# Split input-projection weights kept in DRAM after their first use, in a hybrid decoder layer

## The chip, the core and the metric

The kernel runs on one core of one Trainium2 chip. The metric is the device time of one execution in microseconds (us); less is better. The engines are named as the profile names them: PE is TensorE's matmul, PEld its weight load, DVE is VectorE, ACT is ScalarE, POOL is GpSimd, and SP is the queue that issues every DMA of this kernel.

## The reference

One decoder layer on a sequence of 2048 tokens with a width of 1024, all in float32. The input is normalised, one projection `w_in` makes 4224 columns of it, three branches use the columns, and one output projection adds their result to the input.

```python
h = rmsnorm(x, norm_g[l])
p = h @ w_in[l]
q, k, v, z_att, cb, cc, ch, z_conv, rw_p, z_rwkv = split_cols(p, sizes)
att = diff_attention(...)                    # 4 heads, two softmax maps each
cv = short_conv(cb, cc, ch, conv_w[l])
rw = rwkv7_time_mix(rw_p, ...)               # 4 heads of 64, recurrent
mixed = concatenate([att * silu(z_att), cv * silu(z_conv), rw * silu(z_rwkv)])
x = x + mixed @ w_out[l]
return rmsnorm(x, final_norm_g)
```

## The kernel before

**Tiles of the projection.** The 4224 columns are 33 tiles of 128. A tile's weights are `wr`, 128 partitions by 8 blocks by 128 columns, 512 KB. The product keeps float32 accuracy by splitting: `wh` is `wr` rounded to the matmul's type, `wl` is the rest, and `inproj` (L350) does three matmuls for each of 8 blocks, `wh` with the high part of h, `wh` with its low part, and `wl` with the high part (L357 to L359). One chunk is 512 tokens, so a tile and a chunk are 24 matmuls.

**Loads.** `load_w` (L333) fetches `wr` by one DMA (L326) and splits it: `wh` on ACT in the first stage (L340) and on POOL later (L343, two halves), `wl` on POOL always (L345, four quarters). `wr` has one buffer after the first stage; `wh` and `wl` have two each, so a tile's weights can be made while the tile ahead of it is used.

**How often.** The sequence is worked through in two halves of two chunks. Where a step list is run by `each`, one load serves both chunks; where it is run by `both` (L440), all tiles of chunk 0 come first and then all of chunk 1, with a load for each. So there are 85 loads of 33 tiles: 33 first ones and 52 later ones. The first loads are all in half 0. Run by `both` are six rwkv tiles in the first stage, the four tiles of attention head 3 in half 0 (named K3, V3, Q3 and ZA3 below, in this order), one rwkv tile of half 1, and the eight convolution tiles in half 1 (CC0, CH0, CB0, ZC0 and the same with 1).

**Order of the work.** The main line is: a first stage of projection alone, rwkv of half 0, attention of half 0, rwkv of half 1, attention of half 1, the output projection. While the middle four run, `filler` (L1265) feeds projection matmuls, four or five at a time, between theirs. PE's order is fixed by the program. The order on the other engines and on SP's queue comes from a scheduler that places an instruction where its own model says that it can run. Each engine and SP work strictly in that order: a DMA that waits for a semaphore holds all DMAs behind it.

**Names used.** `xt` are loads of x for the row sums of half 1 (L233), `QL`, `QH`, `K`, `V`, `zs` are loads for attention (L923 to L941, L1042), `pk_`, `pq_`, `pza_` are stores of projection results to DRAM (L370, L385), `P` are softmax tiles, L984 and L985 are the score matmuls, L1060 transposes the softmax tiles. `rs` and `hbc` (L304, L261) scale the first stage's results, `G`, `wu`, `bc` are rwkv matmuls.

Of the kernel before, what the change touches and what calls it, by code (L numbers as in the profile page):

```python
# [11 lines left out]
F32 = mybir.dt.float32  # L12
# [11 lines left out]
NK = 8  # L24
# [8 lines left out]
P = 128  # L33
# [112 lines left out]
def trunk(ctx, tc, a, o, phases="RTO"):  # L146
    nc = tc.nc
    mm = nc.tensor.matmul
    dma = nc.sync.dma_start
# [59 lines left out]
    def dtile(name, shape):  # L209
        return dr.tile(list(shape), F32, name=name)  # L210
# [12 lines left out]
    hl = [[None] * NK, [None] * NK]  # L223
# [95 lines left out]
    early_w, early_r = {}, {}  # L319

    def fetch_w(ti):
        if wpool[0] is not None:
            wr = wpool[0].tile([P, NK, P], F32, name="wr0", bufs=3)
        else:
            wr = ap.tile([P, NK, P], F32, name="wr", bufs=WRB)
        dma(wr, a["wt"][ti])  # L326
        return wr

    def parts(n):

        return [slice(i * NK // n, (i + 1) * NK // n) for i in range(n)]

    def load_w(ti):  # L333
        if ti in early_w:
            return early_w.pop(ti)
        wr = early_r.pop(ti) if ti in early_r else fetch_w(ti)
        wh = ap.tile([P, NK, P], F32R, name="wh", bufs=2)
        wl = ap.tile([P, NK, P], F32R, name="wl", bufs=2)
        if wpool[0] is not None or ON_ACT[0]:
            cpy(wh, wr)  # L340
        else:
            for ks in parts(2):
                nc.gpsimd.tensor_scalar(wh[:, ks], wr[:, ks], 1.0, 1.0, ALU.mult, ALU.mult)  # L343
        for ks in parts(4):
            nc.gpsimd.tensor_tensor(wl[:, ks], wr[:, ks], wh[:, ks].bitcast(F32), ALU.subtract)  # L345
        return wh, wl

    later = []

    def inproj(ti, evac, chunks):  # L350
        wh, wl = load_w(ti)
        for c in chunks:
            ps = pj(f"pj{ti}_{c}")
            flush = list(later)
            later.clear()
            n = 0
            for k in range(NK):  # L357
                for lhs, rhs in ((wh, hh), (wh, hl), (wl, hh)):
                    mm(ps, lhs[:, k], rhs[c][k], start=(n == 0), stop=(n == 3 * NK - 1))  # L359
                    n += 1  # L360
                    if n == 3 * NK:
                        evac(c, ps)
                    yield T512
                    if n == 6:
                        for f in flush:
                            f()
# [964 lines left out]
    with tc.tile_pool(name="st", bufs=1, side="right", reuse_waits="tile") as sp:  # L1331
        wpool[0] = sp
        r = rwkv_steps(0)
        order = (6, 2, 0, 4, 3, 1, 5)
        early_w[T_RW + order[0]] = load_w(T_RW + order[0])
        x0 = load_h0(0, sp)
        for i in order[1:3]:
# [4 lines left out]
        n = 0  # L1342
# [40 lines left out]
        for c in range(2):  # L1383
            for i, (f, args) in enumerate(two):
                ti = (T_RW + order[R0C], T_ZR)[i]
                if c == 0:
                    ws[ti] = load_w(ti)
                early_w[ti] = ws[ti]
                for _ in f(*args, (c,)):
                    pass  # L1390
# [19 lines left out]
    if "mix" in o:  # L1410
        for k in range(8):
            n = 256 if k < 4 else 512
# [43 lines left out]
```

## Time and profile before

| what | us |
|---|---|
| median of 3 runs | 1668.31 (1664.82 to 1672.17) |
| the profiled execution, its own time | 1671.53 |
| span of the profiled execution | 1669.4 |
| PE busy | 1547.7 |
| DVE busy | 948.0 |
| ACT busy | 743.6 |
| POOL busy | 669.9 |

The page slices the span into 40 parts and groups instructions by source line; the other views list an engine's instructions in time, who waited for whom, and the chain of work that ended last. A number in brackets behind a row, such as [2.63 <-DVE P L1030], is the idle time just ahead of the instruction and what ended it.

### The profile page before, as it was taken

What the parts mean: (1) busy time and instruction counts of PE and PEld (TensorE: products, weight loads), DVE (VectorE), ACT (ScalarE), POOL (GpSimd) and SP (SyncE); (2) the same over time, 40 slices, a digit from 0 to 9 for tenths busy, and PEclk for the clock granted to TensorE, in tenths of its full rate; (3) what the DMA queues carried; (4) which work ended last, traced back from release to release, by engine and by line L of the source; (5) the groups of instructions that cost most, each with busy time, mean ns of one, the idle gap of its engine ahead of it and who ended that gap; (6) DMA issues with size and microseconds to landing.
All of it is one profiled execution on the core that took longest, in us unless ns stands there. A gap on an engine that the chain in (4) does not pass through costs nothing.

```text
span 1669.4 us, 29369 instructions
## 1 busy us (share of the span) xinstructions
PE 1547.7 (93%) x10328; PEld 1209.9 (72%) x10328; DVE 948.0 (57%) x2355; ACT 743.6 (45%) x1903; POOL 669.9 (40%) x943
## 2 busy tenths in 40 slices
PE   5999999999998789999999999999989999997998
PEld 4777667677776667887666666778778878876786
DVE  7554765555325866763565554418776766666611
ACT  6432222322216555652322222216656777777732
POOL 4673534333234554344333223235543432321243
PEclk9999999999999898999999999999999999999999
DMA  6324222322266553324323222263343443331233
GB/s 220 101 89 147 61 71 67 89 82 89 76 196 207 174 188 103 98 77 134 98 87 97 80 82 78 79 196 101 111 127 98 145 143 99 109 101 37 73 101 114
DMA packets 147347, 184.70 MB, mean 111 GB/s; under 512 B 39520, under 2 KB 91776, under 8 KB 147200
## 3 DMA queue, kind: packets, MB, share of 16 engines
q1 hardware_dynamic: 147200, 182.82, 35.9%
q8 instruction: 82, 1.34, 0.3%
q14 instruction: 65, 0.53, 0.1%
HBM read 129.26 MB, written 53.48 MB: 109 GB/s over the span
## 4 chain that ended last, share of the span: by engine, by line
PE 54%; DVE 12%; DMA 7%; issue 6%; SPq 5%; POOL 4%; ACT 4%; DVEq 0%; POOLq 0%; ACTq 0%
PE pj L359 24%; PE ops L1232 8%; PE av L1052 6%; PE aT L1060 3%; PE S L984 2%; PE S L985 2%; POOL wl L345 2%; DMA wr<-in_wt_dram 2%; SPq L627 1%; DVE nm L990 1%; DVE tmpx L682 1%; DVE P L1030 1%; SPq L692 1%; DMA U<-ud 1%; ACT P L993 1%
## 5 line engine op out<-in xcount | busy, mean ns | idle before, releaser
L359 PE MATMUL pj<-hh,wh 128*128 128x512 f32 x1008 | 420.9, 418 | 16.8 <-POOL wh L343 11.6
L359 PE MATMUL pj<-hh,wl 128*128 128x512 f32 x1008 | 418.4, 415 | 0.7 <-POOL wl L345 0.5
L359 PE MATMUL pj<-hl,wh 128*128 128x512 f32 x1008 | 418.1, 415 | 0.0
L345 POOL TENSOR_TENSOR wl<-wr,wh 128x256 fp32r<-128x256 f32 x340 | 274.6, 837 | 46.2 <-ACT wh L340 44.1
L993 ACT ACTIVATE P<-S,nm 128x512 f32<-128x512 f32 (+3 forms) x320 | 200.2, 627 | 131.1 <-DVE nm L990 120.8
L990 DVE TENSOR_REDUCE nm<-S 128x1 f32<-128x512 f32 (+3 forms) x320 | 192.7, 607 | 82.3 <-PE S L985 78.7
L359 PEld LDWEIGHTS pj<-hh,wh 128*128 128x128 f32 x1008 | 192.8, 191 | 57.5 <-POOL wh L343 12.9
L359 PEld LDWEIGHTS pj<-hh,wl 128*128 128x128 f32 x1008 | 192.7, 191 | 42.9 <-issue 3.4
L359 PEld LDWEIGHTS pj<-hl,wh 128*128 128x128 f32 x1008 | 192.5, 191 | 39.2 <-issue 2.9
L343 POOL TENSOR_SCALAR wh<-wr 128x512 fp32r<-128x512 f32 x140 | 88.7, 651 | 233.7 <-PE pj L359 148.8
L1052 PE MATMUL av<-aTf,V 128*128 128x256 f32 x576 | 150.8, 386 | 0.0
L984 PE MATMUL S<-K,QH 128*128 128x512 f32 (+2 forms) x320 | 125.3, 392 | 26.7 <-ACT P L993 26.2
L1030 DVE SCALAR_TENSOR_TENSOR P<-P,sc 128x512 f32<-128x512 f32 (+3 forms) x160 | 114.2, 745 | 20.0 <-ACT P L1020 13.2
L985 PE MATMUL S<-K,QL 128*128 128x512 f32 (+2 forms) x320 | 118.5, 370 | 0.0
L1052 PEld LDWEIGHTS av<-aTf,V 128*128 128x128 f32 x576 | 103.0, 193 | 10.8
L1232 PE MATMUL ops<-woh,wh 128*128 128x512 f32 x256 | 105.1, 410 | 5.5 <-ACT wh L1211 5.5
L1065 ACT COPY aTf<-aT 128x512 f32<-128x512 f32 x144 | 84.0, 586 | 57.3 <-PE aT L1060 56.9
L1232 PE MATMUL ops<-wol,wh 128*128 128x512 f32 x256 | 106.1, 414 | 0.0
L1232 PE MATMUL ops<-woh,wl 128*128 128x512 f32 x256 | 105.4, 412 | 0.0
L989 DVE TENSOR_TENSOR S<-S,bt 128x256 f32<-128x256 f32 (+1 forms) x152 | 57.4, 378 | 80.8 <-PE S L985 77.3
L984 PEld LDWEIGHTS S<-K,QH 128*128 128x128 f32 x320 | 61.7, 193 | 51.0 <-ACT P L993 36.6
L1060 PE MATMUL aT<-con,P 128*128 128x128 f32 x576 | 89.6, 279 | 9.5 <-DVE P L1030 5.6
(337 smaller groups left out, 2471.3 us busy)
## 6 DMA issues: line engine op xcount, KB each, us to landing
wr<-in_wt_dram SPq DMA_DIRECT2D x85, 512.0 KB, 3.8
wr<-mx SPq DMA_DIRECT2D x128, 64.0 KB, 2.0
oxt<-in_x_dram SPq DMA_DIRECT2D x32, 256.0 KB, 3.1
out_dram<-oxt SPq DMA_DIRECT2D x32, 256.0 KB, 2.2
prw<-s SPq DMA_DIRECT2D x28, 256.0 KB, 2.0
V<-pv SPq DMA_DIRECT2D x24, 256.0 KB, 3.1
x<-in_xT_dram SPq DMA_DIRECT2D x16, 256.0 KB, 6.5
pv<-t SPq DMA_DIRECT2D x16, 256.0 KB, 2.1
```

What stands on the lines that cost most here:

```text
L343: nc.gpsimd.tensor_scalar(wh[:, ks], wr[:, ks], 1.0, 1.0, ALU.mult, ALU.mult)
L345: nc.gpsimd.tensor_tensor(wl[:, ks], wr[:, ks], wh[:, ks].bitcast(F32), ALU.subtract)
L359: mm(ps, lhs[:, k], rhs[c][k], start=(n == 0), stop=(n == 3 * NK - 1))
L984: mm(s[:, 0:sw], QH[:, m, off:off + P], K[:, m, 0:sw], start=True, stop=False)
L985: mm(s[:, 0:sw], QL[:, m, off:off + P], K[:, m, 0:sw], start=False, stop=True)
L990: nc.vector.tensor_reduce(nm[:, m, g:g + 1], s[:, 0:gw], AX.X, ALU.max, negate=True)
L993: act(p[:, 0:gw], s[:, 0:gw], AF.Exp, bias=nm[:, m, g:g + 1], accum_out=l[:, m, g:g + 1])
L1030: stt(pt[1, g][:, 0:gw], pt[1, g][:, 0:gw], sc[:, 1, g:g + 1], pt[0, g][:, 0:gw], ALU.mult, ALU.add)
L1052: mm(av[:, 0:256], Vs.get((h, kc))[:, ko:ko + P], tf[:, d * 256:d * 256 + 256], start=kb + d == 0, stop=kb + d == nb - 1)
L1060: nc.tensor.transpose(t[:, d * 256 + qi * P:d * 256 + qi * P + P], x["A"][g][:, ko:ko + P], ident)
L1065: cpy(tf, t)
L1232: mm(ps, l[:, k], Ws[n][r][k], start=(c == 0), stop=(c == 3 * NK - 1))
```

## The change

When a tile has been split for the first time, `wh` and `wl` are stored to two DRAM tiles (1 MB together). A later load of the same tile is two DMAs from there straight into `wh` and `wl`; it has no `wr`, and neither ACT nor POOL does anything for it.

```diff
+    wd = {}
+
     def load_w(ti):
+
         if ti in early_w:
             return early_w.pop(ti)
-        wr = early_r.pop(ti) if ti in early_r else fetch_w(ti)
         wh = ap.tile([P, NK, P], F32R, name="wh", bufs=2)
         wl = ap.tile([P, NK, P], F32R, name="wl", bufs=2)
+        if ti in wd:
+            for t, d in zip((wh, wl), wd[ti]):
+                dma(t.bitcast(F32), d)
+            return wh, wl
+        wr = early_r.pop(ti) if ti in early_r else fetch_w(ti)
         if wpool[0] is not None or ON_ACT[0]:
...
         for ks in parts(4):
             nc.gpsimd.tensor_tensor(wl[:, ks], wr[:, ks], wh[:, ks].bitcast(F32), ALU.subtract)
+        wd[ti] = [dtile(f"w{n}{ti}", (P, NK, P)) for n in "hl"]
+        for t, d in zip((wh, wl), wd[ti]):
+            dma(d, t.bitcast(F32))
         return wh, wl
```

In the changed program L355 is the store of a part, L343 its load, and every line behind the edit has a number higher by 10. PE's order is the same before and after. SP's order is not, and neither is POOL's.

SP's queue at the first load of V3 (`wr`, L326), in half 0 of attention, before. The rows ahead are for the tile ZA2 and attention, those behind are the loads of `QH` and `xt`:

```order
L370 DMA pza_0_5352<-th 128x512
L941 DMA QL_5139<-pq_1l 64x256
L326 DMA wr<-in_wt_dram 128x1024
L940 DMA QH<-pq_1h 64x256 x2
L233 DMA xt<-in_x_dram 128x512 x2
```

The same queue after the change, ahead of the same load of V3; `wl_5585` is the stored low part of K3:

```order
L355 DMA wl_5585<-wl 128x1024
L950 DMA QH<-pq_1h 64x256
L233 DMA xt<-in_x_dram 128x512
L950 DMA QH<-pq_1h 64x256
L233 DMA xt<-in_x_dram 128x512 x3
L950 DMA QH<-pq_1h 64x256
L951 DMA QL_5217<-pq_1l 64x256
L233 DMA xt<-in_x_dram 128x512 x2
L950 DMA QH<-pq_1h 64x256 x2
L233 DMA xt<-in_x_dram 128x512
L951 DMA QL_5218<-pq_1l 64x256
L233 DMA xt<-in_x_dram 128x512
```

In these twelve rows stand eleven of the `xt` loads, and no load of weights. The queue goes on with V3's load and what is behind it, and the store of a result for attention:

```order
L950 DMA QH<-pq_1h 64x256 x2
L233 DMA xt<-in_x_dram 128x512 x3
L951 DMA QL_5218<-pq_1l 64x256
L326 DMA wr<-in_wt_dram 128x1024
L395 DMA pk_0h<-thi 128x512
```

The load of V3 stood ahead of all sixteen `xt` loads and the `QH` loads among them; it now stands behind them, in the place that Q3's load had.

SP's queue where attention of half 1 begins, before. The second `wr` is CC0's load; the 21 loads of `K`, `QH`, `QL` and `V` begin behind it:

```order
L326 DMA wr<-in_wt_dram 128x1024
L370 DMA pv_2_12116<-t_12114 128x512
L370 DMA pv_3_12253<-t_12251 128x512
L830 DMA mx_3_139<-Y 128x256
L326 DMA wr<-in_wt_dram 128x1024
L923 DMA K<-pk_0h 64x512
L924 DMA K<-pk_0l 64x512
```

The same queue after the change, at the end of those 21 loads; `wh_1264` and `wl_1265` are CC0's stored parts, `wh_1362` and `wl_1363` are CH0's:

```order
L939 DMA V<-pv_0_3370 128x512
L395 DMA pq_2h<-thi 128x512
L395 DMA pq_2l<-tlo 128x512
L395 DMA pq_3h<-thi 128x512
L395 DMA pq_3l<-tlo 128x512
L380 DMA pza_2_12317<-th 128x512
L343 DMA wh<-wh_1264 128x1024
L343 DMA wl<-wl_1265 128x1024
L380 DMA pza_3_12347<-th 128x512
L343 DMA wh<-wh_1362 128x1024
L343 DMA wl<-wl_1363 128x1024
```

CC0's load stood ahead of the 21 loads; it now stands behind them and behind five stores.

SP's queue where CH0 is loaded for its second chunk, after the change:

```order
L343 DMA wh<-wh_1362 128x1024
L1196 DMA wor<-in_wo_dram 128x512 x5
L951 DMA QL_12205<-pq_2l 64x256
L493 DMA mx_2_130<-th 128x512
L950 DMA QH<-pq_2h 64x256 x2
L1196 DMA wor<-in_wo_dram 128x512
L950 DMA QH<-pq_2h 64x256 x2
L1196 DMA wor<-in_wo_dram 128x512 x2
L951 DMA QL_12205<-pq_2l 64x256
L343 DMA wl<-wl_1363 128x1024
```

Fourteen DMAs came between the two halves of this load.

## Rows read from the trace of the kernel before

**Rows 1.** The page's part 1: engine, busy us, share of the span, instructions.
```profile
PE 1547.7 (93%) x10328; PEld 1209.9 (72%) x10328; DVE 948.0 (57%) x2355; ACT 743.6 (45%) x1903; POOL 669.9 (40%) x943
```
**Rows 2.** Busy us (and instructions) of PE, PEld, DVE, ACT, POOL; PEclk, DMA share, GB/s.
```profile
0.00:20.00 20.00, 10.57 (x32) 6.44 (x33) 12.72 (x21) 15.86 (x26) 8.91 (x19) 1.00 0.88 306
...
480.00:645.00 165.00, 135.93 (x600) 108.79 (x599) 103.27 (x243) 86.30 (x234) 80.45 (x112) 0.90 0.60 183
```
**Rows 3.** Groups of the two POOL splits: busy us, mean ns of one, idle before.
```profile
L345 POOL TENSOR_TENSOR wl<-wr,wh 128x256 fp32r<-128x256 f32 x340 | 274.6, 837 | 46.2 <-ACT wh L340 44.1 <-PE pj L359 2.2
...
L343 POOL TENSOR_SCALAR wh<-wr 128x512 fp32r<-128x512 f32 x140 | 88.7, 651 | 233.7 <-PE pj L359 148.8 <-DMA wr<-in_wt_dram 71.4 <-DMA K<-pk_3l 8.3
```
**Rows 4.** Waits of PE, whole span: us in total, times, longest us.
```profile
PE pj L359 <- POOL wh L343: 11.6, 3, 5.5
```
**Rows 5.** Waits of PE in 600 to 660, 780 to 1060 and 1130 to 1300 us.
```profile
PE S L984 <- ACT P L993: 5.8, 2, 3.3
...
PE G L607 <- DVE KB L595: 3.1, 2, 1.6
PE wu L755 <- DVE Z L747: 2.7, 3, 1.5
...
PE S L984 <- ACT P L993: 7.1, 6, 3.7
```
**Rows 6.** SP's queue in time around V3's load: start us, us, engine line operation.
```profile
498.68 0.33 SPq L326 DMA_DIRECT2D wr<-in_wt_dram  x1
...
517.36 0.45 SPq L941 DMA_DIRECT2D QL<-pq_1l  x1
517.90 0.54 SPq L326 DMA_DIRECT2D wr<-in_wt_dram  x1
```
**Rows 7.** POOL in time: the split of the tile whose load was issued at 517.90.
```profile
523.42 1.20 POOL L343 TENSOR_SCALAR wh<-wr 128x512 fp32r<-128x512 f32 x2 [5.38 <-DMA wr<-in_wt_dram]
```
**Rows 8.** PE in time: V3's first matmul, two idle times behind it.
```profile
512.39 0.58 PE L359 MATMUL pj<-hh,wh 128*128 128x512 f32 x1
...
525.22 0.55 PE L1060 MATMUL aT<-con,P 128*128 128x128 f32 x3 [2.63 <-DVE P L1030]
...
568.67 0.79 PE L359 MATMUL pj<-hh,wh 128*128 128x512 f32 x1 [5.54 <-POOL wh L343]
```
**Rows 9.** SP's queue in time where attention of half 1 begins.
```profile
1091.41 0.37 SPq L326 DMA_DIRECT2D wr<-in_wt_dram  x1
...
1105.52 0.58 SPq L929 DMA_DIRECT2D V<-pv  x1
...
1108.31 0.52 SPq L370 DMA_DIRECT2D pza<-th  x1
1108.92 0.76 SPq L326 DMA_DIRECT2D wr<-in_wt_dram  x1
```
**Rows 10.** PE in time: the first matmul of CC0, and that of CH0.
```profile
1108.08 0.39 PE L359 MATMUL pj<-hh,wh 128*128 128x512 f32 x1
...
1117.51 0.79 PE L359 MATMUL pj<-hh,wh 128*128 128x512 f32 x1 [3.67 <-POOL wh L343]
```
**Rows 11.** The chain that ended last: start us, us, what.
```profile
1108.92 7.77 DMA wr<-in_wt_dram
```
**Rows 12.** SP's queue in time: the load ahead of CH0's second `wl`.
```profile
1200.99 0.55 SPq L941 DMA_DIRECT2D QL<-pq_2l  x1
```
**Rows 13.** PE in time: CH0's second chunk, its first matmul with `wl`.
```profile
1201.77 0.40 PE L359 MATMUL pj<-hh,wl 128*128 128x512 f32 x1
```
**Rows 14.** DMA of the whole span: packets; then issues, KB each, median us to landing.
```profile
DMA packets 147347, 184.70 MB, mean 111 GB/s; under 512 B 39520, under 2 KB 91776, under 8 KB 147200
...
wr<-in_wt_dram SPq DMA_DIRECT2D x85, 512.0 KB, 3.8
```
**Rows 15.** L242 on DVE: duration ns min/median/max, first and last start us.
```profile
L242 DVE SCALAR_TENSOR_TENSOR x<-x,gn,ccs x16: 740/1222/1784, 60.6 to 91.9; 128x512 f32<-128x512 f32 x16
L242 DVE SCALAR_TENSOR_TENSOR xk<-xk,vec,ccs x16: 735/744/1708, 552.5 to 622.2; 128x512 f32<-128x512 f32 x16
```

## The prediction

> **What bounds the kernel now.** First the page's part 1: PE is busy 93% of the span, and POOL, whose work the change removes, 40% [rows 1]. So removed POOL work helps only where PE waits for it, directly or through others. Next the groups by line: the two splits cost POOL 837 ns for each quarter of `wl` and 651 ns for each half of `wh` [rows 3]. Then the waits of PE: the projection waits for POOL's `wh` three times in the whole span, 11.6 us in all [rows 4]; the other waits are for ACT and DVE in attention and rwkv [rows 5]. Then stretches of time: the worst for PE is 480 to 645 us, where 136 of 165 us are busy, the granted clock is 0.90, and DMA runs at a share of 0.60 [rows 2]. The reader should see two things: a large removal that PE hardly waits for, and a stretch in which PE is late already and that the order of SP's queue changes. The places where the queue changes are then read in time, on SP, POOL and PE [rows 6 to 13].
>
> **What is removed and added.** A later load makes four quarters of `wl` no more: 52 x 4 x 0.837 = 174 us of POOL. Six of the later loads are in the first stage, where ACT makes `wh`; the other 46 drop two halves each, 46 x 2 x 0.651 = 60 us. POOL loses about 234 of its 670 us. On the other side, a first load adds two stores of 512 KB (33 MB-sized pairs, 34.6 MB) and a later load adds one DMA of 512 KB (52, 27.3 MB): 61.9 MB on top of 184.7, so about 247 MB, and 118 more DMAs on SP. PE's instructions and order stay.
>
> The sum is made against the profiled execution, 1671.53 us, which lies 3.2 above the median of 1668.31.
>
> **Term 1, V3's first load.** Before, it was issued at 498.68 and V3's first matmul ran at 512.39 without a wait [rows 6, 8]. Now it stands behind the `QL` load that was issued at 517.36, in a place where before a load went out at 517.90 [rows 6]. The split of that load began at 523.42, 5.52 after the issue, and a half takes 0.60 [rows 7]. So V3's first matmul comes at about 517.90 + 5.52 + 0.60 = 524.0, which is 11.6 late. Behind it PE already waited 2.63 for DVE [rows 8], and DVE goes on while PE stands: 11.6 - 2.6 = **+9.0**. Bounds: between the two places stand 28 DMAs of some 0.5 us [rows 6]; if none of them waits, the load goes out at 512.7, and with the median landing of 3.8 [rows 14] the delay is 4.7 and the term +2. With the longest landing in view, 7.77 [rows 11], and nothing made good behind it, it is 13.9, say +15 with SP also held by the stores of K3 ahead of it.
>
> **Term 2, V3's second load.** It cost 5.54 us of PE time at 568.67 [rows 8]. It keeps its place on SP, loses the split (0.6), and its `wl` is a second 512 KB that is needed two matmuls later. I take **-1**; bounds -3 (landing at the median) and +2 (`wl` late).
>
> **Term 3, CC0 and CH0.** CC0's load went out at 1091.41, ahead of 21 loads [rows 9], and CC0 began at 1108.08 without a wait [rows 10]. Now it stands behind them and behind stores, where CH0's load was: issued at 1108.92 [rows 9], landed 7.77 later by the chain [rows 11], so at 1116.7. That is 8.6 late. CH0's wait of 3.67 [rows 10] goes, since its load follows two DMAs behind and now has CC0's whole delay as cover. **+4.9**. Bounds: with the median landing of 3.8 it is +1; with `wl` later still, +6.5.
>
> **Term 4, CH0's second chunk.** Its `wl` now stands behind the `QL` that was issued at 1200.99 [rows 12]: issue 1201.5, landed at 1205.3 with 3.8 [rows 14]. The first matmul that wants it ran at 1201.77 [rows 13]. The delay is 3.6; attention waits for ACT in the same stretch [rows 5] and makes part of it good. I take **+2**, bounds 0 and +5.
>
> **Term 5, relief of the other engines.** The trace shows that DVE is slower while POOL works: L242, the same operation on the same shape, takes 1222 ns at the median in the first stage, where POOL splits without a pause, and 744 ns later [rows 15]. That is 39% off where POOL is taken away. The waits of PE that hang on such DVE work, directly or through ACT, are 5.8, 3.1, 2.7 and 7.1, together 18.7 us [rows 5]; 39% of these is **-7**. Bounds: 0 (the waits are chains that POOL doesn't slow) and -18.7 (all go).
> The Trainium skill, page "SBUF — State Buffer", section "Who interferes with whom", says that a DVE instruction with two SBUF inputs contends with a GpSimd instruction that reads SBUF, and that the one issued second is blocked. The 1222 against 744 ns agrees. By this rule the relief is real wherever a split was removed, but it says nothing of whether PE was waiting.
>
> **Term 6, traffic.** Stores fall heaviest where a tile is loaded first, and the first 20 us run at a DMA share of 0.88 and 306 GB/s already [rows 2]. A 512 KB transfer at that rate takes 1.7 us. I take one such delay, **+2**; bounds 0 and +10 (six of them).
> The Trainium skill, page "DMA: Bandwidth & Descriptors", section "Latency and other measured facts", speaks against the change here: it gives 0.2 us for an access to HBM on average and 2 us under high load. Worked out from that page, an estimate, a later load under load would land up to 1.8 us later than a median one, and terms 1, 3 and 4 would come to some 5 us more. The row shows a median landing of 3.8 us for 512 KB and one of 7.77 [rows 11, 14], so spread is there, though no run here shows its cause.
>
> **Sum.** 9.0 - 1 + 4.9 + 2 - 7 + 2 = +9.9 on the profiled execution, 1681.4; against the median, 1668.3 + 9.9 = **1678 us**. The 234 us of POOL count for nothing beyond term 5, since POOL was off PE's path except for the 11.6 us [rows 4], of which 9.2 are in terms 2 and 3.
>
> **Rivals.**
> - **A, hidden.** The other engines catch up during the new waits, and SP reaches the loads early. Terms at their kind ends (1: +2, 3: +1, 4: 0), 2 at -1, 5 at -7, 6 at +2: -3, so 1665, and 1662 to 1671 around it. For it: SP's place on the clock depends on buffers that PE frees. Against it: V3's load is behind all sixteen `xt` loads.
> - **B, DMA saturates.** In 480 to 645 us the DMA share of 0.60 [rows 2] rises with stores and double loads, and every load there comes late. All terms at their bad ends (15 + 2 + 6.5 + 5 + 0 + 10) are +38.5; halfway between the sum and that is +24, so 1692, range 1684 to 1698. Against it: the mean over the span is only 111 GB/s [rows 14].
> - **C, faster by the relief.** DVE is freed, all 18.7 us of the waits in term 5 go, and terms 1 to 4 stay at their kind ends (+2, -3, +1, 0): -18.7, so 1650, range 1646 to 1660. It decides at V3's load: if SP issues it before 512.39 - 6.1 = 506.3 us, V3 waits for nothing. For it: L242's ratio [rows 15]. Against it: the trace shows SP at 517 there [rows 6].
> - **Nothing happens** is excluded: the order of SP's queue shows the later loads reading the stored parts.
>
> **How the numbers follow.** About 0.5% (8.3 us) is what a measurement of this kernel can tell from no change, so the marks are 1660 and 1676.6. The forecast case, +3 to +15 or 1671 to 1683, has a chance of 0.42; some 60% of it lies above 1676.6: slower 0.25, same 0.17. A has 0.23, all same. B has 0.15, slower. C has 0.20, faster. So faster 0.20, same 0.40, slower 0.40. The range leaves out the fast half of C (0.1) and the slow half of B (0.08): 1654 to 1692. The forecast's own range is 1671 to 1683.
>
> **What would show it.** POOL's busy time near 436 us and 247 MB moved follow from the counts. Term 1 is right if PE waits some 9 to 12 us at V3's first matmul, and wrong if less than 4. Term 3: a wait of about 8 us at CC0 and none at CH0. Term 4: a wait of some 3.5 us for a DMA of `wl` in CH0's second chunk. Term 2: V3's second wait near 5, and for a DMA. Term 5: L242 in the first stage near 744 ns and a shorter sum of PE's waits for ACT's `P`; if the splits go and L242 keeps 1222, it is wrong. Term 6: more time from issue to landing for small loads. The whole falls if SP reaches V3's load before 506 us (then C), or if new waits appear at tiles that are not named here (then B).

## The result and the profile after

Five runs of the changed kernel have a median of 1683.87 us (1678.10 to 1690.22), five of the kernel before 1668.63 us (1664.82 to 1672.17). The ratio is 1.0090, with a 95% interval of 1.0062 to 1.0119: slower by some 15 us. The forecast was 1678, in a range of 1654 to 1692.

The profiled execution of the changed kernel took 1690.22 us, the longest of its five; that of before took 1671.53. Their difference is 18.7 us, so what is summed below is some 3.5 us more than the medians say. The page's part 1 of the changed kernel (engine, busy us, share, instructions), against [rows 1]:

```profile
PE 1552.1 (92%) x10328; PEld 1214.4 (72%) x10328; DVE 915.5 (54%) x2355; ACT 739.3 (44%) x1897; POOL 446.2 (26%) x643
DMA packets 164339, 246.57 MB, mean 146 GB/s; under 512 B 41408, under 2 KB 93664, under 8 KB 164192
```

POOL fell by 224 us, where 234 were counted, and the bytes rose by 61.9 MB, as counted. DVE fell by 32 us, though none of its instructions was taken away. PE's busy time rose by 4 us with the same matmuls, at a mean granted clock of 0.973 against 0.980.

Busy time of PE, PEld, DVE, ACT and POOL in two stretches, with the clock, the DMA share and GB/s; first the changed kernel, then the one row of before that [rows 2] does not have:

```profile
20.00:60.00 40.00, 31.92 (x133) 24.81 (x132) 23.33 (x32) 17.50 (x39) 18.01 (x19) 0.93 0.93 338
480.00:650.00 170.00, 129.03 (x574) 103.63 (x573) 93.75 (x222) 82.92 (x221) 47.70 (x65) 0.89 0.73 234
```
```profile
20.00:60.00 40.00, 32.06 (x137) 25.46 (x135) 22.50 (x32) 18.52 (x39) 20.94 (x23) 0.91 0.40 136
```

From 20 to 60 us the DMA share goes from 0.40 to 0.93, and PE is as busy as before: that stretch has room. From 480 us the share goes from 0.60 [rows 2] to 0.73, and there PE loses time.

The waits of PE in the whole span of the changed kernel: us in total, times, longest. They answer to [rows 4].

```profile
PE S L994 <- ACT P L1003: 20.2, 18, 2.5
PE pj L369 <- POOL wh L350: 17.9, 2, 11.9
PE pj L369 <- DMA wh<-wh: 13.2, 4, 6.1
PE wu L765 <- DVE Z L757: 7.6, 7, 1.6
...
PE pj L369 <- DMA wl<-wl: 5.2, 2, 4.7
...
PE S L994 <- DMA QH<-pq_1h: 4.4, 1, 4.4
```

The three waits of before for POOL (11.6 us) became two (17.9), and 18.4 us of waits for the reloads themselves are new, beside one of 4.4 for `QH`.

PE's instructions are the same in both kernels and stand in the same order, so each can be matched with itself: its start in one kernel less its start in before is the delay that has gathered up to there. The table gives this in us for the profiled executions, each time for the last matmul that started ahead of the time named, which is a time of before; 506, 514 and 548 lie around V3's first matmul, 1106 to 1130 around CC0 and CH0, 1200 to 1300 around CH0's second chunk. The experiments of the next section are in it too.

| kernel | 200 | 480 | 506 | 514 | 548 | 640 | 1060 | 1116 | 1130 | 1207 | 1300 | 1660 |
|---|---|---|---|---|---|---|---|---|---|---|---|---|
| the change | -3.0 | 4.3 | 9.3 | 21.8 | 18.2 | 15.7 | 10.2 | 19.1 | 14.2 | 23.4 | 20.7 | 19.1 |
| x1 stores only | -2.3 | 0.8 | 6.1 | 18.5 | 15.6 | 18.4 | 17.2 | 17.2 | 15.6 | 16.5 | 18.0 | 14.2 |
| x2 one pair stored | -7.6 | -7.4 | -7.6 | -8.2 | -8.2 | -11.3 | -16.0 | -8.1 | -11.8 | -3.8 | -8.1 | -7.6 |
| x3 loads early | -6.0 | -1.3 | -4.7 | -1.0 | 0.0 | -7.0 | -2.0 | -2.0 | -4.2 | -5.6 | -6.0 | -7.3 |
| x4 before, loads early | 0.6 | 1.0 | -2.4 | -1.6 | -3.9 | -5.4 | -4.1 | -4.1 | -11.1 | -10.7 | -7.9 | -10.5 |
| x5 V3 early | -3.8 | 2.0 | 8.0 | 11.4 | 13.4 | 15.2 | 12.6 | 21.4 | 16.9 | 23.7 | 19.4 | 18.1 |
| x6 x3, split again | -5.8 | 1.4 | -2.1 | 0.1 | 0.4 | -2.1 | 21.5 | 21.4 | 18.3 | 18.1 | 25.3 | 24.2 |
| x7 nine tiles, early | -4.7 | -3.3 | -6.8 | -5.4 | -7.8 | -11.4 | -6.5 | -6.2 | -13.1 | -13.0 | -10.4 | -13.9 |
| x8 POOL issues stores | 2.4 | 24.9 | 28.7 | 26.6 | 29.6 | 26.0 | 21.5 | 29.2 | 27.2 | 34.1 | 29.8 | 27.3 |
| x9 x3, POOL issues | 1.6 | 21.1 | 17.6 | 20.6 | 24.0 | 21.3 | 27.5 | 27.5 | 23.3 | 22.5 | 22.2 | 20.9 |
| x10 x7, POOL issues | -0.6 | 1.7 | -1.7 | -1.6 | -2.1 | -2.9 | 2.6 | 2.6 | -4.4 | -2.5 | 0.8 | -2.0 |
| x11 nine, first loads early | -6.1 | -4.8 | -8.3 | -6.7 | -7.0 | -7.0 | -0.6 | -0.2 | -7.2 | -7.5 | -5.2 | -4.1 |
| x12 five not stored | -5.9 | -1.3 | 3.1 | 13.6 | 10.2 | 5.9 | 0.3 | 11.5 | 10.3 | 18.4 | 15.6 | 13.5 |

The change loses 7 us from 200 to 480, 17 at 480 to 514, 9 at CC0 and 11 at CH0's second chunk (12.2 at 1200), and gets back a part behind each. Five matmuls at which it loses most, in PE's own order of time, with the idle time ahead and what ended it (the first is ZA2's, the third V3's, then CC0's, and CH0's with `wl`):

```profile
494.04 0.79 PE L369 MATMUL pj<-hh,wh 128*128 128x512 f32 x1 [6.01 <-POOL wh L350]
...
519.24 0.76 PE L994 MATMUL S<-K,QH 128*128 128x512 f32 x1 [4.41 <-DMA QH<-pq_1h]
...
534.57 0.79 PE L369 MATMUL pj<-hh,wh 128*128 128x512 f32 x1 [11.86 <-POOL wh L350]
...
1124.44 0.77 PE L369 MATMUL pj<-hh,wh 128*128 128x512 f32 x1 [6.08 <-DMA wh<-wh]
...
1221.83 0.80 PE L369 MATMUL pj<-hh,wl 128*128 128x512 f32 x1 [4.74 <-DMA wl<-wl]
```

V3's row names POOL, but POOL had been idle: SP issued the load only here (start us, us), against 498.68 before [rows 6], and the matmul came 7.28 us behind the issue.

```profile
526.78 0.45 SPq L951 DMA_DIRECT2D QL<-pq_1l  x1
527.29 0.58 SPq L326 DMA_DIRECT2D wr<-in_wt_dram  x1
```

### The profile page after: what moved, and what is told of

Same layout as the page of the kernel before. It is cut to its first block, busy times and chain, and to the rows that moved or that the text cites. A ratio compares the mean times of both kernels' runs of the same rounds, so it can differ in the third digit from the quotient of the medians.

```text
span 1688.4 us, 29212 instructions
## 1 busy us (share of the span) xinstructions
PE 1552.1 (92%) x10328; PEld 1214.4 (72%) x10328; DVE 915.5 (54%) x2355; ACT 739.3 (44%) x1897; POOL 446.2 (26%) x643
## 4 chain that ended last, share of the span: by engine, by line
PE 59%; DVE 13%; DMA 12%; SPq 7%; ACT 4%; issue 4%; POOL 1%; DVEq 0%; POOLq 0%; ACTq 0%
PE pj L369 27%; PE ops L1242 8%; PE av L1062 6%; PE aT L1070 3%; PE S L994 3%; PE S L995 3%; SPq L637 2%; SPq L702 2%; DVE tmpx L692 2%; DMA U<-ud 1%; DVE nm L1000 1%; DMA zd<-Zs 1%; ACT P L1003 1%; DMA wl<-wl 1%; SPq L639 1%
## 5 line engine op out<-in xcount | busy, mean ns | idle before, releaser
L369 PE MATMUL pj<-hh,wh 128*128 128x512 f32 x1008 | 422.2, 419 | 34.7 <-POOL wh L350 17.9
L369 PEld LDWEIGHTS pj<-hh,wh 128*128 128x128 f32 x1008 | 193.5, 192 | 76.3 <-POOL wh L350 18.7
L994 PE MATMUL S<-K,QH 128*128 128x512 f32 (+2 forms) x320 | 125.6, 392 | 24.7 <-ACT P L1003 20.2
L352 POOL TENSOR_TENSOR wl<-wr,wh 128x256 fp32r<-128x256 f32 x132 | 106.0, 834 | 47.5 <-ACT wh L347 41.9
L1040 DVE SCALAR_TENSOR_TENSOR P<-P,sc 128x512 f32<-128x512 f32 (+3 forms) x160 | 105.6, 692 | 19.3 <-ACT P L1030 16.1
L1062 PEld LDWEIGHTS av<-aTf,V 128*128 128x128 f32 x576 | 103.5, 194 | 11.4 <-ACT aTf L1075 0.6
L994 PEld LDWEIGHTS S<-K,QH 128*128 128x128 f32 x320 | 61.9, 193 | 47.4 <-ACT P L1003 29.6
L1030 ACT ACTIVATE P<-P,sc 128x512 f32<-128x512 f32 (+3 forms) x144 | 87.5, 664 | 13.6 <-DVE sc L1022 13.0
```

Of the source, the lines that this page charges most:

```text
L994: mm(s[:, 0:sw], QH[:, m, off:off + P], K[:, m, 0:sw], start=True, stop=False)
L1030: act(pt[0, g][:, 0:gw], pt[0, g][:, 0:gw], AF.Copy, scale=sc[:, 0, g:g + 1])
L1040: stt(pt[1, g][:, 0:gw], pt[1, g][:, 0:gw], sc[:, 1, g:g + 1], pt[0, g][:, 0:gw], ALU.mult, ALU.add)
L1062: mm(av[:, 0:256], Vs.get((h, kc))[:, ko:ko + P], tf[:, d * 256:d * 256 + 256], start=kb + d == 0, stop=kb + d == nb - 1)
```

## The experiments

All ratios are to the kernel before, run on the same chip beside them, with their 95% intervals.

| run | median us | ratio | interval |
|---|---|---|---|
| x1 stores only | 1684.20 | 1.0071 | 1.0046 to 1.0096 |
| x2 one pair stored | 1663.81 | 0.9952 | 0.9936 to 0.9967 |
| x3 loads early | 1664.54 | 0.9955 | 0.9934 to 0.9975 |
| x4 before, loads early | 1662.64 | 0.9947 | 0.9923 to 0.9972 |
| x5 V3 early | 1683.49 | 1.0074 | 1.0048 to 1.0101 |
| x6 x3, split again | 1695.58 | 1.0148 | 1.0104 to 1.0191 |
| x7 nine tiles, early | 1657.29 | 0.9915 | 0.9889 to 0.9941 |
| x8 POOL issues stores | 1693.12 | 1.0140 | 1.0113 to 1.0167 |
| x9 x3, POOL issues stores | 1696.95 | 1.0160 | 1.0124 to 1.0195 |
| x10 x7, POOL issues stores | 1667.00 | 0.9970 | 0.9951 to 0.9988 |
| x11 nine tiles, first loads early | 1663.60 | 0.9941 | 0.9913 to 0.9969 |
| x12 five not stored | 1683.91 | 1.0073 | 1.0056 to 1.0090 |

**The theory** after the result: the place of a few loads in SP's queue decides. **The rival**: the extra bytes decide, wherever they are.

**x1, the stores alone.** Against the change:

```diff
-        if ti in wd:
-            for t, d in zip((wh, wl), wd[ti]):
-                dma(t.bitcast(F32), d)
-            return wh, wl
...
+        if ti in wd:
+            return wh, wl
         wd[ti] = [dtile(f"w{n}{ti}", (P, NK, P)) for n in "hl"]
```

> The parts of a first load are stored as in the change, but later loads fetch the unsplit weights and split them again, so only the 33 pairs of stores (34.6 MB) are added. The order of SP's queue has V3's first load as late as in the change, and CC0's and CH0's as early as before. Theory (the place of late loads decides): V3 waits 10 to 12 us as in the change, no wait at CC0, CH0's wait of 3.7 and the slower DVE of before come back, so about the offset that the change has at 640 us, +16 against before; 1684, at least 1678. Rival (the extra bytes decide): 56% of the bytes, so 56% of the change's +15: +8, 1677, spread over the whole span rather than at V3.

The ratio is 1.0071. The waits for POOL's `wh` are 29.5 us in 480 to 660 us, with 15.1 at V3 (waits of PE in that stretch). The loss is all gathered by 514 us (+18.5) and nothing is lost at CC0 or CH0.

```profile
PE pj L367 <- POOL wh L346: 29.5, 3, 15.1
```

So the stores, with the late place that V3's load has beside them, are enough for the loss at V3, and the reloads alone have to do with CC0 and CH0.

**x2, the reloads alone.** Only the first tile is stored, and all later loads read its parts:

```diff
+        if wd:
+            wd[ti] = next(iter(wd.values()))
+            return wh, wl
         wd[ti] = [dtile(f"w{n}{ti}", (P, NK, P)) for n in "hl"]
```

> Only the first tile's parts are stored, and every later load of any tile reads these two parts (so the projections after it use one tile's weights, and the output is another): the reloads of the change without 32 of its 33 pairs of stores. V3's first load then stands as early as before, CC0's and CH0's as late as in the change. Theory (place): no 10 us wait at V3, the wait of some 6 us at CC0 and of some 5 us for a low part in CH0 remain, the relief of the other engines remains: about 0 against before, 1664 to 1672. Rival (bytes): 44% of the bytes, +7, 1675.

The ratio is 0.9952: faster than before, and just below the theory's figure. From 200 to 506 us nothing is lost (-7.6 to -7.6), V3 has no wait, and the waits at CC0 and at CH0's `wl` stand, as these rows of 1080 to 1300 us show (waits of PE):

```profile
PE pj L372 <- DMA wh<-wh: 7.2, 2, 5.5
PE pj L372 <- DMA wl<-wl: 5.2, 1, 5.2
```

**x3 and x4, the loads moved forward.** The same edit in the change (x3) and in the kernel before (x4, which has the first line alone). It lets the scheduler take a load ahead of other work, and changes no instruction:

```diff
-        dma(wr, a["wt"][ti])
+        with nullcontext() if wpool[0] is not None else tc.high_priority(500):
+            dma(wr, a["wt"][ti])
...
-                dma(t.bitcast(F32), d)
+                with nullcontext() if wpool[0] is not None else tc.high_priority(500):
+                    dma(t.bitcast(F32), d)
```

> The change, with every load of projection weights after the first stage given precedence on SP's queue, so that V3's, CC0's and both of CH0's loads go out earlier; bytes, splits and stores as in the change. Theory (place): the waits at V3 (11.9), CC0 (6.1) and CH0's low part (4.7) shrink to under 2 each, about -18 with the clock, so 1664 to 1670. Rival (bytes): no change against the changed kernel, 1684, the waits only turn up at other loads.

> The kernel before with the same precedence for its loads: the control for x3. Theory (place): before has few late loads; its waits at V3's second load (5.5), ZA2 (2.4) and CH0 (3.7) shrink in part: -3 to -8, 1660 to 1665. Rival (bytes): same as before, 1668. If x3 is below x4, dropping the splits is worth something by itself; if it is above by 5 or more, the extra traffic costs that.

x3 has all the bytes of the change and comes out at 0.9955. The bytes as such do not decide. Its waits of PE in 480 to 560 us, which for the changed kernel hold V3's 11.86:

```profile
PE S L996 <- DMA QH<-pq_1h: 7.5, 2, 4.5
PE pj L371 <- DVE mn L1016: 1.4, 1, 1.4
```

V3 waits no more; two loads of `QH` are late instead, and the delay falls by 5.7 from 480 to 640 us. Against that stands x4: the kernel before gains as much by the same edit, 0.9947. So with the loads well placed the change is worth nothing in the whole that these runs can tell. In the table x3 stands 6.6 us ahead of x4 at 200 us; it loses 4.3 of that by 480, where the stores fall, and 3.7 from 640 to 1060.

**x5, V3's load alone.**

```diff
-        dma(wr, a["wt"][ti])
+        with tc.high_priority(500) if ti == T_V + 3 else nullcontext():
+            dma(wr, a["wt"][ti])
```

> The change, with precedence on SP's queue for one load alone, V3's first; every other load as the scheduler places it in the change. Theory: the wait of 11.9 us at V3 shrinks to under 3, CC0's 6.1 and CH0's 4.7 stay; before the stage the change is +9, so +9 less the relief, about -10 against the changed kernel: 1674 (1670 to 1677). Rival (the wait moves on to the next load, since one buffer holds all unsplit weights): within 4 us of the changed kernel, 1680 to 1684.

The theory falls in this form: the ratio is 1.0074, and 1683.49 us is the rival's figure. SP issues V3's load at 511.34 and V3 waits for nothing, but from 480 to 640 us the delay grows by 13.2, as much as in the change (11.4). The waits of PE in 480 to 560 us:

```profile
PE pj L370 <- POOL wh L351: 8.0, 3, 6.5
PE S L995 <- DMA QH<-pq_1h: 7.5, 1, 7.5
PE pj L370 <- POOL wl L353: 2.1, 2, 1.5
```

The wait moved on, to `QH`, though not for the buffer that the rival named. `QH` is late by its own place. In before, the load that this matmul needs goes out right behind another load of `QH` (both between 499.06 and 500.71 us, ahead of all sixteen `xt`). In the change, eight DMAs stand between the two: two stores of parts, five `xt` loads and a store of `pza`. It goes out 3.5 us later than the delay of 9.3 so far explains, and the matmul comes 6.3 us behind the issue. In x5 ten DMAs stand between, V3's load among them; it goes out at 514.49, and the matmul comes 6.5 us later. SP's queue in the change (start us, us):

```profile
507.77 0.45 SPq L950 DMA_DIRECT2D QH<-pq_1h  x1
508.31 0.54 SPq L355 DMA_DIRECT2D wh<-wh  x1
508.90 2.02 SPq L233 DMA_DIRECT2D xt<-in_x_dram  x3
511.02 0.38 SPq L380 DMA_DIRECT2D pza<-th  x1
511.44 0.95 SPq L233 DMA_DIRECT2D xt<-in_x_dram  x2
512.49 0.42 SPq L355 DMA_DIRECT2D wl<-wl  x1
512.96 0.50 SPq L950 DMA_DIRECT2D QH<-pq_1h  x1
...
535.12 0.32 SPq L355 DMA_DIRECT2D wh<-wh  x1
```

(With these five, eight in the first listing of the section on the change, not eleven, and three in the second, the `xt` loads ahead of V3's are sixteen.)

A second explanation, theory A, came from what SP waits for at the head of its queue in the change, from 490 to 540 us (us, times, longest): a store of `wh` (L355) that POOL has not made yet.

```profile
SPq L355 <- POOL wh L350: 6.2, 1, 6.2
```

Theory A says that such stores hold the loads behind them. Rival B was that the stores' bytes cost it, and rival C that V3's place costs it with or without stores. But this wait ends at 535.12, in the last row above: it is the store of V3's own `wh`, and stands behind V3's load (527.29) and `QH`, so it made neither late. From 480 to 528 us SP waited for a part not yet made only once, 0.5 us. What the stores cost in this stretch they cost by their turns in the queue, and by the places that other loads get beside them. Theory A can bear only on the stretch ahead, where SP does wait for such stores (waits of SP in 200 to 480 us):

```profile
SPq L355 <- POOL wh L350: 34.3, 10, 8.5
...
SPq L355 <- POOL wl L352: 15.3, 10, 3.3
```

**x6, the splits made again.** x3, with POOL's old six instructions for each tile that is reloaded after the first stage (nearly all in half 1), into a scratch tile:

```diff
+            if wpool[0] is None:
+                wr = ap.tile([P, NK, P], F32, name="wr", bufs=WRB)
+                for ks in parts(2):
+                    nc.gpsimd.tensor_scalar(wr[:, ks], wh[:, ks].bitcast(F32), 1.0, 1.0, ALU.mult, ALU.mult)
+                for ks in parts(4):
+                    nc.gpsimd.tensor_tensor(wr[:, ks], wh[:, ks].bitcast(F32), wl[:, ks].bitcast(F32), ALU.subtract)
             return wh, wl
```

> The kernel of x3, but in half 1 POOL does its old six instructions for every reloaded tile again, into a scratch tile that nobody reads (46 tiles, 234 less the first stage's 20 us); loads, stores and their order as in x3. It takes the relief of term 5 away and leaves the rest. Theory (relief is real, some 0.4 of PE's waits on DVE and ACT): +4 to +8 against x3, 1669 to 1672. Rival (POOL's work never mattered behind the first stage): within 2 us of x3, 1663 to 1667.

It cost far more than either figure: 1.0148, of which 23.6 us from 640 to 1060. But POOL also stood still for the reloads there, 63.6 us (waits of POOL in 640 to 1060 us), with rwkv's POOL work queued behind:

```profile
POOL wr L349 <- DMA wh<-wh: 63.6, 19, 13.4
```

So the run adds a wait beside the work, and its time does not tell what POOL's work alone costs. PE's four waits of [rows 5] tell part of it: at the same matmuls they come to 11.9 us in x3 and 17.8 here (more under term 5).

**x7, nine tiles.** x3, but only the nine rwkv tiles of the first stage are stored and read back:

```diff
+        if wpool[0] is None:
+            return wh, wl
         wd[ti] = [dtile(f"w{n}{ti}", (P, NK, P)) for n in "hl"]
```

> The kernel of x3, but only the nine rwkv tiles of the first stage are stored and read back (16 later loads: six in the first stage, ten in half 1); the other 24 tiles are loaded and split as before, so 9 pairs of stores instead of 33 and no extra traffic in the stages with attention. Theory: the gain of placement that x4 shows (-8.5) and the relief of the first stage (-3 to -5) add up: 1656 to 1660, below x3 and x4. Rival (the reloads in attention were what x3 gained by): 1662 to 1665, as x4 or worse.

1657.29 us, a ratio of 0.9915, the fastest of all: the gain of the first stage (-4.7 at 200 us, where x4 has +0.6) and that of the placement. Its interval overlaps that of x4 (from 0.9923 to 0.9941), so that it beats x4 is likely and not shown.

**x8 to x10, POOL issues the stores.** The same edit in the change, in x3 and in x7:

```diff
         for t, d in zip((wh, wl), wd[ti]):
-            dma(d, t.bitcast(F32))
+            nc.gpsimd.dma_start(d, t.bitcast(F32))
```

> The change, with the 66 stores of the parts issued by POOL, which has just made them, instead of SP. Bytes, splits and reloads as in the change; V3's first load is back in its old place, CC0's and CH0's stay late. Theory A (a store that waits for POOL at the head of SP's queue holds the loads and QH behind it): no wait over 4 us at V3 or for QH in 490 to 530 us, the offset to before at 640 us falls from +16 to between -8 and 0, the end at 1664 to 1671. Rival B (the stores' bytes on the DMA engines cost it, whoever issues them): within 4 us of the change, 1680 to 1687.

> x3 (all late loads given precedence) with the stores issued by POOL. Theory A: the two waits for QH that x3 still has (4.5 and 3.0 us near 505 to 512) go, and the 4 us that x3 loses in 300 to 360 us go if they too are SP's, and stay if they are the bytes': 1656 to 1661, against 1664.5 for x3. Rival B: as x3, 1662 to 1667.

> x7 (nine tiles kept, precedence for the loads) with its 18 stores issued by POOL. All of them fall in the first stage and shortly behind it, where x7 shows no wait that a store causes but the late scale of the first stage (4.1 us). Theory A: 0 to -3 against x7, 1654 to 1657. Rival B: the same as x7.

All three are slower than their fellows with SP, and both figures for the whole were missed: 1.0140, 1.0160 and 0.9970. In x8 the delay grows by only 1.1 us from 480 to 640 us (24.9 to 26.0), V3 waits for nothing, and no wait for `QH` is over 3.0. But V3's load is back in its old place there, so this does not tell theory A from rival C. And 24.6 us were lost ahead of it, from 125 to 480 us (0.3 to 24.9), where rwkv of half 0 runs and where the change loses 7.1. SP waits for no store there, so by theory A alone x8 should have lost less. DVE waited there for rwkv's small loads of `Z` 23.1 us in x8, against 12.2 in the change (waits of DVE in 130 to 480 us, both):

```profile
DVE X L714 <- DMA Z<-zd: 23.1, 7, 4.2
```
```profile
DVE X L714 <- DMA Z<-zd: 12.2, 6, 4.6
```

These are idle times of DVE, 11 us more than in the change, beside 17.5 us more of delay; how much of them reached PE, and what made the rest, stays open.

**x11, precedence for first loads alone.** x7 with the second hunk of x3's edit undone:

```diff
-                with nullcontext() if wpool[0] is not None else tc.high_priority(500):
-                    dma(t.bitcast(F32), d)
+                dma(t.bitcast(F32), d)
```

> x7 (nine rwkv tiles kept), with precedence only for loads of unsplit weights; the reloads of kept parts go where the scheduler puts them. In rwkv of half 1 (640 to 1060 us) the kernels whose reloads have precedence lost 5 us against before (x3, x7) and those without gained 5 (the change, x2). Theory (an early reload holds back the small loads that rwkv waits for): that stretch goes from +5 to -4, and the whole to 1649 to 1653. Rival (chance of the scheduler's order, not precedence): as x7, 1656 to 1659.

The theory falls. From 640 to 1060 us x11 goes from -7.0 to -0.6, a loss of 6.4, when x7 lost 4.9. The whole is 0.9941, not better than x7. Why rwkv of half 1 gains 5 us in the change, in x2 and in x12, and loses as much in x3, x7 and x11, is open.

**x12, no stores in the stretch.** The change, with the five tiles first loaded there left out of the keeping:

```diff
+        if ti in (T_ZA + 2, T_K + 3, T_V + 3, T_Q + 3, T_ZA + 3):
+            return wh, wl
         wd[ti] = [dtile(f"w{n}{ti}", (P, NK, P)) for n in "hl"]
```

> The change, but the five tiles first loaded in 480 to 570 us (ZA2, K3, V3, Q3, ZA3) are not stored and are split again later: no store stands in SP's queue in that stretch, while V3's first load is still placed behind the sixteen loads of x. Theory A (stores that wait for POOL at the head of SP's queue cost the stretch): SP comes to V3's load sooner, V3 waits under 6 us, the offset grows by at most 4 from 480 to 640 us instead of 11, and the end is 1671 to 1677. Rival C (the place in the order alone costs it): V3 waits 9 us or more, the offset grows by 9 or more, 1680 to 1686.

Rival C holds for V3: no store of a part stands in SP's queue there, and V3, still placed behind the sixteen loads of `x`, waits longer than in the change (PE in time):

```profile
526.37 0.80 PE L371 MATMUL pj<-hh,wh 128*128 128x512 f32 x1 [12.67 <-POOL wh L350]
```

The load went out at 519.53 and the matmul came 6.84 us later. The delay grows by 14.9 to 514 us and by 7.2 to 640, where theory A allowed 4 and C asked for 9, so in size it lies between. Together, x5 and x12 show two causes of which each costs the stretch: V3's late place with no stores (x12: +7.2), and stores as the change has them, with the late `QH` and V3's load moved forward (x5: +13.2). With neither, the stretch gains (x2: -3.9; x4: -6.4). It gains in x3 as well, which keeps the stores but has every load of weights earlier. That SP waits for stores is not what parts x3 from the change: it waits for none in this stretch of x3, and for 0.5 us ahead of V3's load in the change.

## Why the prediction was right, and where its sizes were off

The direction and the mechanism held: loads that the change makes late decide, and POOL's 224 us count for little. The direction was held weakly: slower and no change had the same chance, 0.40, and the 1683.87 us lie inside the wide range (1654 to 1692) but just outside the forecast's own, 1671 to 1683. Term by term, in the delays of the table (profiled executions):

- **Term 1, V3's first load.** Forecast: 11.6 late, 2.6 made good, +9.0. The delay goes from +10.4 just ahead to +22.2 at the matched matmul, so 11.8; by 548 us it is 18.2, so +7.8 is left. Right in place and cause: x12 shows the place to be enough. In size two small errors met: the load went out 1 us earlier than forecast (527.29 less the 10.4 is 516.9, not 517.90), and the matmul came 7.28 behind it, not 6.12. What the term did not say is that the stretch would be no faster with V3 moved (x5), since SP's queue there had a second late load.
- **Term 2.** Forecast: -1. V3's second load makes PE wait 3.32 us for its DMA, where it was 5.54 for POOL [rows 8]; the delay falls there from 20.5 to 18.2, so -2.2, within the bounds. The same 2.2 were lost just ahead of it, so between 548 and 572 us the delay only goes from 18.2 to 18.1.
- **Term 3, CC0 and CH0.** Forecast: 8.6 late, 3.67 regained, +4.9. Measured: +9.0 from 1106 to 1116, and +4.1 left at 1130. x2 has it too, without the stores, and x1 does not, and CH0's own wait is gone, as forecast: right in place and cause. That the size fits is in part luck. The wait is 6.08, not 8.6; most of the rest is work at the clock's lower level (1.2 GHz), which the term did not have: after the wait the granted clock is 0.51 from 1123 to 1130 us, where before had 1.00 at the same matmuls (1108 to 1114 us).
- **Term 4, CH0's second chunk.** Forecast: 3.6 late, +2 left. This term was mis-sized: +11.2 at 1207 (12.2 to 23.4) and +8.5 left at 1300. SP issued the `wl` at 1216.58, 2.9 us later than the forecast's 1201.5 when the 12.2 gathered so far are taken off (fifteen DMAs, not fourteen, stood between the two halves, and SP itself stood still for 2.7 us among them); and the matmul came 5.2 us behind the issue, where the median landing of 3.8 [rows 14] was taken. Of the 11.2, 2.7 were lost just ahead, most of it in a wait for ACT's `P` (1.86), and the wait for `wl` is 4.74. The rest, 3.8, goes with the clock: PE ran at the lower level around the wait, as the stretch of 1215 to 1229 us shows (columns as above, clock 0.51), where before had 1.00 from 1201 to 1209. By an estimate that cost half of the 9.26 us of busy time there, some 4.6, part of it ahead of the wait:

```profile
1215.00:1229.00 14.00, 9.26 (x24) 6.96 (x25) 9.06 (x17) 8.84 (x22) 5.12 (x5) 0.51 0.51 167
```

- **Term 5, relief.** Forecast: -7, with L242 near 744 ns as the sign. L242 in the first stage went from 1222 [rows 15] to 746 (durations min, median, max):

```profile
L242 DVE SCALAR_TENSOR_TENSOR x<-x,gn,ccs x16: 736/746/1561, 59.4 to 85.1; 128x512 f32<-128x512 f32 x16
```

  In x1, which keeps the splits, it is 1222 again. The four waits that the term was worked out from, 18.7 us [rows 5], come to 13.9 in the changed kernel (PE in 616 to 676, 790 to 1070 and 1144 to 1321 us, the same matmuls):

```profile
PE S L994 <- ACT P L1003: 3.9, 2, 2.3
...
PE wu L765 <- DVE Z L757: 3.2, 3, 1.5
...
PE G L617 <- DVE KB L605: 1.5, 2, 1.0
...
PE S L994 <- ACT P L1003: 5.3, 4, 2.5
```

  So 4.8 went, a quarter of them and not 39%. That it goes with the splits shows in all fourteen profiles: at the same matmuls these waits come to 10.0 to 13.9 us in the seven kernels that read kept parts in half 1 (the change, x2, x3, x5, x8, x9, x12) and to 17.0 to 20.2 in the seven that split all or most tiles there (before, x1, x4, x6, x7, x10, x11). The delay itself fell by 3.0 us up to 200 us and by 5.5 from 640 to 1060, together 8.5. That this is near 7 is luck: the first stage was not in the term, and x1 has 2.3 of its 3.0 without any relief. And the relief need not reach the whole: x3 has it and still loses 5.0 from 640 to 1060.
- **Term 6, traffic.** Forecast: +2, at most +10. This is the other step that failed in size: from 200 us to just ahead of V3 the delay went from -3.0 to +10.4, so 13.4. Three waits carry 8.8 of it: rwkv's `wu` for DVE (4.3 us against 1.4 of before, in 200 to 510 us), ZA2's for POOL (6.0 against 2.4), and `QH` (4.4, where PE had waited 2.1 at this matmul before). x2, without the stores, has 0.0 there up to 506 us, so the stores make it. I had priced one late transfer at 1.7 us, by its bytes; what the stores do to the other DMAs of the queue was not in the price. For ZA2 and `QH` it is their place: ZA2's load, too, now goes out behind a store of `wl` and a store of `pq_`, 2.5 us later than the delay so far explains. For the part up to 480 us the way is open: SP waited 49.6 us there for parts to be stored (rows under x5), and bytes were added too; the wait of `wu` is 1.2 to 1.6 us from 200 to 480 in the kernels with no stores there (before, x2, x4, x7) and 2.9 to 4.3 with them (the change, x1, x3, x12).

The terms as measured: 8.5 regained in term 5's two stretches, and 13.4 + 7.8 - 0.1 + 4.1 + 8.5 = 33.7 lost, less 6.1 of small gains elsewhere, is the +19.1 of the table's end. Terms 6 and 4 were too small by 11.4 and 6.5; the small gains, which no term had, and the other terms gave half of that back, and the forecast came out 6 us low against the median and 9 against the profile. So the total is nearer than its parts, by luck.

Rival A (hidden) did not come true in size, but its mechanism is there at V3: of the 22.2 at V3 the change has 15.7 left at 640 us, x12 comes down from 13.6 to 5.9, and x5, without V3's wait, is no better over the stretch. Rival B (DMA saturates) is ruled out as what decides by x3, with the same bytes and 0.79 of DMA share in 480 to 640 us, faster than before. Rival C (faster by the relief) named the right condition, that V3's load be issued in time: x3 meets it and comes out faster, though x4, which gains as much without any relief, speaks against the relief as what the whole gains by.

The Trainium skill, page "DMA: Bandwidth & Descriptors", section "Latency and other measured facts", gives an access to HBM 0.2 us on average and 2 us under high load. The landings of the changed kernel do rise: 4.9 us at the median for its 33 loads of unsplit weights, where before has 3.9 for its loads in the same stretch (up to 575 us) and 3.8 for all 85 [rows 14]; no run shows whether HBM is the cause. x3 has 5.1 and is fast, so longer landings alone did not make the change slow.

## What to carry to other kernels

Taking work off an engine that the critical engine hardly waits for is worth little, and what the change adds to a queue in strict order can cost more: here, with 66 stores and 52 more loads on one issuing queue, a handful of loads came so late that PE waited 4 to 12 us for each. Compare the order of the issuing queue before and after the edit, look for the loads that moved behind a burst, and price them at the times of the trace; then see whether placement alone, without the edit, gives the same gain (x4 did). Where a result is kept for reuse, try keeping only what is first loaded in a stretch that has room (x7, the fastest run, though not shown to beat x4).

## What the runs showed that I had not expected

- Two late causes in one stretch hide each other. Moving V3's load forward took away a wait of 11.9 us and gained nothing (x5); taking the stretch's stores away left 7.2 of its 11.4 us (x12). It gained only where neither was there (x2, x4), or where every load of weights was early (x3).
- The same stores issued by POOL landed, at the median, 5.6 (`wh`) and 6.3 us (`wl`) behind their issue, where SP's took 3.2 in the change, and rwkv of half 0 lost 25 us (x8) where it lost 7 with SP as the issuer.
- The longest wait of SP for a store in the stretch around V3 was a consequence of V3's late load and not its cause. A list of waits does not tell the order in time; the timeline does.
- A wait of 4.74 us went with a delay of 11.2, some 4.6 of it (an estimate) since the clock was at its lower level around it.
- The kernel before gains 0.5% by the order of its loads alone (x4).
